# Hybrid pool and mLSTM decode layer on one core: products reordered between units, input copied for the combinations, more row tiles in the heads

## Chip, cores and metric

The kernel runs on one core of a Trainium2 chip. The metric is the device time of one execution in microseconds (us). TensorE is PE in the rows, VectorE DVE, ScalarE ACT, GpSimd POOL, SyncE SP.

## What is computed

One layer on 560 rows of 1024 values: 16 meta tokens and 512 prompt tokens, and 8 sequences of 4 sample tokens. All is fp32. Shortened from the reference:

```python
hn = rmsnorm(x, norm_g)
a_pool, z_pool, q, k, v, o, z_m, i_pre, f_pre, g_pool, g_mlstm = split(hn @ w_in)
y_pool = multiscale_pool(pool_buf, a_pool, w_pool, pool_scale) * silu(z_pool)
# mLSTM, 4 heads of 512: gates ig, lf = log_sigmoid(f); running maximum m
s   = (q @ k.T) * w_intra
num = s @ v + w_inter * (q @ C)
den = sum(s) + w_inter * (q @ n)
h   = num / max(abs(den), exp(-m_t))
C_new = decay * C + (k * w_state).T @ v
y_mlstm = sigmoid(o) * head_norm(h) * silu(z_m)
u = sigmoid(g_pool) * (y_pool @ w_branch_pool) + sigmoid(g_mlstm) * (y_mlstm @ w_branch_mlstm)
y = rmsnorm(x + u @ w_out, final_g)
```

## The kernel before

Each fp32 operand is split into a high part, rounded to fp32r, and the rest, `lo`; a product is three fp32r matmuls (`mm3`, line 161). The hidden rows stand transposed in `hT_hi` and `hT_lo`, 128 by 8 by 560.

**Front.** `begin` normalises five row tiles, transposes them, copies the high part out of the transposes' PSUM banks on ScalarE, subtracts for the low part on VectorE (`parts`, line 445), and runs the first input projection (`project`, line 464) on tiles 0 and 1, then on the others. `projections_begin` (660) weaves three step lists into the v units of head 0 (`unit_v`, 949): the gate weights' products and the gate chain (`gates`, 560), and `quarter_sums` (531).

**Combinations.** Most column blocks of the input projection are *quad* units (`quad`, 186): a two by two block product with seven products p1, p2, p6, p5, p7, p3, p4 in place of eight. They need four combinations S a to d of quarters of the hidden rows. `quarter_sums` rebuilds the input as `hT_hi + hT_lo` on GpSimd (line 539), eight times in two rounds, adds and subtracts on VectorE (542), and splits into high (ScalarE, 549) and low parts (547, b and d on GpSimd). A unit combines its weights too: `ahead` loads `ra` and `rb`, casts `w1` and `w2`, adds, casts `wa` and `wb`, and subtracts the low parts on VectorE.

**Order.** In `projections` (687) the program writes the order of TensorE by hand: unit after unit, each with the next unit's `ahead` steps, the previous unit's `after` steps and the update of the sample state (C) woven in. p2 and p7 to p4 accumulate in PSUM banks which a unit's own evictions (`keep`, `total`) free: p1 into bank A, kept by ScalarE (238), then p6 into A; VectorE forms q, zx and so on from the banks (251, 253, 255), and p4 is the last product in A.

**Heads.** `attention` (1201) runs four heads: scores of query and key, weights P, `key_sums` (D, then its split dh and dl, 1411 to 1416), `numerator` (sqn and og, 1449 to 1456), `variances`, a square root and a reciprocal, and `scaled` (1470), which multiplies og by D and stores it. D, four og and four sqn of a head come from the tag `row` with 9 tiles (1255). `rows` are the products for C_prompt (1358, 1359), called prompt_C below. Then come the pool branch (`yp`, loaded by `y_in`, 1497), the mLSTM branch and the output product.

Of the kernel before, what the change touches and what calls it, by code (L numbers as in the profile page):

```python
# [8 lines left out]
F32 = mybir.dt.float32  # L9
F32R = mybir.dt.float32r  # L10
AF = mybir.ActivationFunctionType
ALU = mybir.AluOpType
# [4 lines left out]
P = 128  # L17
# [66 lines left out]
class Unit:  # L84
# [3 lines left out]
    def __init__(self, load=(), ahead=(), products=(), after=(), then=()):  # L88
        self.load, self.ahead, self.products = list(load), list(ahead), list(products)
        self.after, self.then = list(after), list(then)  # L90


# [7 lines left out]
class Trunk:  # L100
# [85 lines left out]
    def quad(self, src, lo, dst, scale=None, f21=None, after=(), then=()):  # L186
# [94 lines left out]
        def p4():  # L281
            product("A", cols("wb", 0), quarter(1, 1), False)
            for out, c0, c1, how in w["dst"]["21"]:
                A.activation(out, view(w["A"], c0, c1, how), f21 or AF.Copy, scale=1.0 if scale is None else scale)
        return Unit([load], ahead, [p1, p2, p6, p5, p7, p3, p4], after, then)

# [76 lines left out]
    def begin(self):  # L363
# [28 lines left out]
        V.tensor_copy(self.ones, self.ones32)  # L392
        self.hT = [ip.tile([P, NK, NT], F32R, name=n) for n in ("hT_hi", "hT_lo")]
        self.hS = ip.tile([P, NK, 112], F32R, name="hS")
        self.acol = mp.tile([P, 5, H], F32, name="acol")
# [49 lines left out]
        def parts(*js):  # L445
            pieces = []
            for j in js:
                for q in range(2):
                    pv = pss[j, q].rearrange("p (k t) -> p k t", k=4)
                    for s, n, c0 in COLS[j]:  # L450
                        pieces.append((pv[:, :, s:s + n], *(t[:, 4 * q:4 * q + 4, c0:c0 + n] for t in self.hT)))
            for src, hi, lo in pieces:
                pA.copy(hi, src)
            for src, hi, lo in pieces:
                pV.tensor_tensor(lo, src, hi.bitcast(F32), ALU.subtract)

        def first(j):
# [73 lines left out]
    def quarter_sums(self):  # L531
        nc = self.nc
        V, A, G = nc.vector, nc.scalar, nc.gpsimd
        steps, x = [], {}

        def load(k0, half, kh):
            t = x[half, kh] = self.gp.tile([P, 2, HN], F32, tag=f"x{half}{kh}", name=self.name("x"), bufs=1)
            hi, lo = (t[:, 4 * kh + k0:4 * kh + k0 + 2, HN * half:HN * half + HN].bitcast(F32) for t in self.hT)
            G.tensor_tensor(t, hi, lo, ALU.add)  # L539

        def sums(op, out, p, q):
            V.tensor_tensor(x[out], x[p], x[q], op)

        def part(k0, s, t, low):
            hi, lo = (u[:, k0:k0 + 2] for u in self.S[s])
            if low:
                (G if s in "bd" else V).tensor_tensor(lo, x[t], hi.bitcast(F32), ALU.subtract)
            else:
                A.copy(hi, x[t])
        a, b, c, d = (1, 1), (0, 0), (1, 0), (0, 1)  # L550
        for k0 in (0, 2):
            steps += [lambda k0=k0, t=t: load(k0, *t) for t in (a, c, b, d)]
            steps += [lambda: sums(ALU.subtract, a, c, a), lambda: sums(ALU.subtract, c, b, c),
                      lambda: sums(ALU.subtract, b, a, b), lambda: sums(ALU.add, d, d, b)]
            for s, t in ("a", a), ("b", b), ("c", c), ("d", d):
                steps += [lambda k0=k0, s=s, t=t, l=l: part(k0, s, t, l) for l in (False, True)]
        return steps


    def gates(self):  # L560
# [21 lines left out]

        V.scalar_tensor_tensor(az, z, -1.0, z, ALU.mult, ALU.max)
        e, u = row("ge"), row("gu")
# [38 lines left out]
        for i in (3, 2, 1, 0):  # L623
            own = TILE0[i] + P - TSTART[i]
            V.tensor_copy(sv[i][:, :own], nQ[:, TSTART[i]:TSTART[i] + own])

            V.tensor_scalar(sv[i][:, own:], sv[i + 1][:, :SEGW[i] - own],
                            b[:, TILE0[i] + P - 1:TILE0[i] + P], None, ALU.add)
            yield
        for i in range(5):  # L630
            c0 = TILE0[i]
            c1 = c0 + (P if i < 4 else 16)
            last = (SEGW[i] if i < 4 else 16) - 1
            V.tensor_scalar(wsr[:, c0:c1], a[:, c0:c1], sv[i][:, last:last + 1], None, ALU.add)
            yield
# [24 lines left out]
    def projections_begin(self):  # L660
# [6 lines left out]
        sums = self.quarter_sums()  # L667
        for f in v[0].ahead + a.products:
            f()
        for n, u in enumerate(v):  # L670
            now = [sums[:len(sums) // (4 - n)], other[:len(other) // (6 - n)]]
            sums, other = sums[len(now[0]):], other[len(now[1]):]
            if n == 2:
                z = self.unit_z(0)
                for f in z.load:
                    f()
            weave(u.products, (v[n + 1] if n < 3 else z).ahead, *now)
# [9 lines left out]
    def projections(self, rest):  # L687
# [45 lines left out]
        self.early = self.head(0)  # L733
        loaded, C, outs = 0, {}, []
        before = Unit(after=rest[0].after + rest[1].after)
# [4 lines left out]
        for t, u in enumerate(units):  # L740
# [20 lines left out]
        for f in before.after + old.then + before.then + outs:  # L761
            f()
# [186 lines left out]
    def unit_v(self, h):  # L949
# [251 lines left out]
    def attention(self):  # L1201
# [15 lines left out]
        for h, u in enumerate(heads):  # L1217
# [21 lines left out]
    def head(self, h):  # L1239
# [256 lines left out]

    def y_in(self, yy, k, src):
        nc = self.nc
        t = self.r("y32")[:, :NO]
        nc.sync.dma_start(t, src)  # L1500
        self.split(yy[0][:, k], yy[1][:, k], t, nc.scalar, nc.gpsimd if k % 2 else nc.vector)
# [11 lines left out]
    def pool_branch(self):  # L1513
# [12 lines left out]
        for k in range(8):  # L1526
            self.y_in(self.yp2, k, self.yp_d[:, k])
        for g in range(4):
# [7 lines left out]
    def final(self, up):  # L1536
# [4 lines left out]
        for m in range(16):  # L1541
            y_in(ym[m // 8], m % 8, self.y_d[:, m])
        fg = fp.tile([P, D], F32, name="fg")
# [95 lines left out]
```

## Time and profile before

| | us |
|---|---|
| three runs | 1145.27, 1148.51, 1151.25 |
| median | 1148.51 |
| profiled execution | 1146.45 |
| its span | 1144.6 |
| TensorE, VectorE, ScalarE, GpSimd busy | 1066.5, 843.0, 533.5, 195.2 |
| granted TensorE clock, mean | 0.97 |

The busy times lie in the span; what the profiled execution takes beyond its span lies around it. An idle time in brackets in a row is that of the engine just before the instruction, with what ended it; idle time counts only where the engine is the one that sets the end. The granted clock is 1.00 at 2.4 GHz and 0.50 at 1.2 GHz.

### The profile page before, as it was taken

What the parts mean: (1) busy time and instruction counts of PE and PEld (TensorE: products, weight loads), DVE (VectorE), ACT (ScalarE), POOL (GpSimd) and SP (SyncE); (2) the same over time, 40 slices, a digit from 0 to 9 for tenths busy, and PEclk for the clock granted to TensorE, in tenths of its full rate; (3) what the DMA queues carried; (4) which work ended last, traced back from release to release, by engine and by line L of the source; (5) the groups of instructions that cost most, each with busy time, mean ns of one, the idle gap of its engine ahead of it and who ended that gap; (6) DMA issues with size and microseconds to landing.
All of it is one profiled execution on the core that took longest, in us unless ns stands there. A gap on an engine that the chain in (4) does not pass through costs nothing.

```text
span 1144.6 us, 19677 instructions
## 1 busy us (share of the span) xinstructions
PE 1066.5 (93%) x7390; PEld 961.5 (84%) x7390; DVE 843.0 (74%) x1346; ACT 533.5 (47%) x1003; POOL 195.2 (17%) x323
## 2 busy tenths in 40 slices
PE   7948999998999999999998999986999789999997
PEld 5848999967999968999868989975978679999976
DVE  5696888796789697889696888863699888534353
ACT  4455555333554435554444554455677555222232
POOL 3720120001210000400001300022454534100000
PEclk9978999998999999999999999997999899999999
DMA  8424456779656778657588567887677699522232
GB/s 214 149 51 122 136 166 203 256 235 275 214 182 219 238 257 236 212 178 249 186 266 262 167 223 268 282 280 259 205 264 248 203 310 353 174 74 75 66 116 83
DMA packets 159663, 233.33 MB, mean 204 GB/s; under 512 B 17369, under 2 KB 82133, under 8 KB 159561
## 3 DMA queue, kind: packets, MB, share of 16 engines
q1 hardware_dynamic: 159569, 232.09, 63.2%
q8 instruction: 58, 0.95, 0.3%
q14 instruction: 36, 0.29, 0.1%
HBM read 160.65 MB, written 70.93 MB: 202 GB/s over the span
## 4 chain that ended last, share of the span: by engine, by line
PE 68%; DMA 11%; DVE 9%; issue 4%; ACT 3%; POOL 3%; SPq 1%; DVEq 0%; POOLq 0%; ACTq 0%
PE ps L166 55%; PE ps L974 4%; DMA v_d<-v 3%; PE ps L1121 2%; DMA wraw<-in_w_in_dram 2%; PE ps L1358 2%; PE ps L1130 1%; DMA kw<-k_d 1%; DMA out_dram<-C 1%; POOL x L539 1%; ACT qc L1156 1%; DMA k<-k_d 1%; PE ps L1401 1%; PE ps L977 1%; DMA ra<-in_w_in_dram 1%
## 5 line engine op out<-in xcount | busy, mean ns | idle before, releaser
L166 PE MATMUL ps<-hT_hi,w 128*128 128x272 f32 (+1 forms) x752 | 159.0, 297 | 0.0
L166 PEld LDWEIGHTS ps<-hT_hi,w 128*128 128x128 f32 x752 | 125.3, 193 | 4.2 <-issue 2.4
L166 PE MATMUL ps<-hT_lo,w 128*128 128x272 f32 (+1 forms) x376 | 110.2, 293 | 0.0
L1135 DVE SCALAR_TENSOR_TENSOR C<-C,sw,ps 128x512 f32<-128x512 f32 x128 | 89.4, 741 | 12.1 <-PE ps L1130 11.8
L166 PE MATMUL ps<-Sb_hi,wb 128*128 128x272 f32 (+1 forms) x376 | 80.9, 295 | 17.5 <-DVE wb L205 15.6
L166 PE MATMUL ps<-hT_hi,wb 128*128 128x272 f32 (+1 forms) x376 | 82.7, 299 | 11.4 <-DVE q L253 7.7
L1044 POOL COPY qm<-qw 128x16 f32<-128x16 f32 x32 | 7.1, 254 | 430.4 <-DVE qw L1041 430.4
L166 PE MATMUL ps<-Sa_hi,wa 128*128 128x272 f32 (+1 forms) x376 | 79.9, 292 | 0.0
L166 PE MATMUL ps<-Sc_hi,wa 128*128 128x272 f32 (+1 forms) x376 | 78.9, 290 | 0.0
L166 PEld LDWEIGHTS ps<-Sb_hi,wb 128*128 128x128 f32 x376 | 63.2, 192 | 18.7 <-issue 16.0
L166 PE MATMUL ps<-Sd_hi,w 128*128 128x272 f32 (+1 forms) x376 | 78.7, 289 | 0.0
L202 ACT CAST wa<-ra 128x1024 fp32r<-128x1024 f32 x47 | 49.4, 1050 | 62.0 <-DVE ra L215 55.4
L205 DVE TENSOR_TENSOR wb<-rb,wb 128x1024 fp32r<-128x1024 f32 x47 | 57.7, 1227 | 24.6 <-ACT wb L202 24.3
L166 PEld LDWEIGHTS ps<-hT_hi,wb 128*128 128x128 f32 x376 | 64.5, 195 | 13.1 <-DVE q L253 8.4
L166 PEld LDWEIGHTS ps<-hT_lo,w 128*128 128x128 f32 x376 | 72.6, 193 | 0.0
L202 ACT CAST w<-rb 128x1024 fp32r<-128x1024 f32 x47 | 49.3, 1050 | 29.3 <-PE ps L166 16.2
L166 PEld LDWEIGHTS ps<-Sa_hi,wa 128*128 128x128 f32 x376 | 63.0, 191 | 0.0
L166 PEld LDWEIGHTS ps<-Sc_hi,wa 128*128 128x128 f32 x376 | 62.2, 189 | 0.0
L166 PEld LDWEIGHTS ps<-Sd_hi,w 128*128 128x128 f32 x376 | 61.9, 188 | 0.0
L205 DVE TENSOR_TENSOR w<-rb,w 128x1024 fp32r<-128x1024 f32 x47 | 57.3, 1220 | 4.3 <-ACT w L202 4.3
L205 DVE TENSOR_TENSOR wa<-ra,wa 128x1024 fp32r<-128x1024 f32 x47 | 57.5, 1224 | 0.0
L166 PE MATMUL ps<-hT_lo,wb 128*128 128x272 f32 (+1 forms) x188 | 55.8, 297 | 0.0
(372 smaller groups left out, 3115.6 us busy)
## 6 DMA issues: line engine op xcount, KB each, us to landing
C<-in_state_C_dram SPq DMA_DIRECT2D x64, 512.0 KB
out_dram<-C SPq DMA_DIRECT2D x64, 512.0 KB
ra<-in_w_in_dram SPq DMA_DIRECT2D x47, 512.0 KB
rb<-in_w_in_dram SPq DMA_DIRECT2D x47, 512.0 KB
wraw<-in_w_in_dram SPq DMA_DIRECT2D x18, 512.0 KB
v<-v_d SPq DMA_DIRECT2D x32, 256.5 KB
wraw<-in_w_branch_mlstm_dram SPq DMA_DIRECT2D x16, 512.0 KB
k_d<-k SPq DMA_DIRECT2D x16, 280.0 KB
```

Source lines behind the costliest of these rows:

```text
L166: self.nc.tensor.matmul(out, s, m, start=(first and j == 0), stop=(j == len(seq) - 1), skip_group_check=not check)
L202: A.copy(w[name][0], w[s])
L205: V.tensor_tensor(w[name][1], w[s], w[name][0].bitcast(F32), ALU.subtract)
L539: G.tensor_tensor(t, hi, lo, ALU.add)
L974: nc.tensor.matmul(pv[i], s, m[:, k2], start=(k == 0 and j == 0), stop=(k == 7 and j == 2))
L977: nc.tensor.matmul(pv[4][:112], self.hS[:, k], m[:, k2], start=(k == 0 and j == 0), stop=(k == 7 and j == 1))
L1121: nc.tensor.matmul(self.pqc[h][r:r + 8], self.qm[h % 2][:, d, b], Cs[bb // 2][:, bb % 2], start=(d == 0 and g == 0), stop=(d == 3 and g == 1),
L1130: nc.tensor.matmul(pu, self.kwst[h, d][r:r + 12, g], self.vst[h][r:r + 12, g], start=True, stop=True, tile_position=(r, 0))
L1135: V.scalar_tensor_tensor(C, C, self.bview(self.sw[h][:, 0])[:, 4 * g + bb, 3:4], pu, ALU.mult, ALU.add)
L1156: A.activation(t[r, :HD], pqc[r], AF.Copy, accum_out=t[r, HD:])
L1358: nc.tensor.matmul(pc, w[:, s, i], vr[i][:, m], start=(i == 0 and j == 0), stop=False)
L1401: nc.tensor.matmul(pb[:, o:o + mv.shape[-1] - m], s, mv[:, m:], start=(j == 0), stop=(j == last[True]))
```

## The change

1. **Tails.** A quad unit's last product, p4, is issued behind the first product of the unit after it, where that unit's first product is an ordinary one.
2. **Input X.** The transposes' banks are copied whole by ScalarE into a tile X, after the high and low parts; `quarter_sums` takes quarters of X, in place. All low parts of S, and those of the first v unit's weights, are VectorE's. Around the gates, the absolute value, four copies and five adds of the gate rows are ScalarE's, and the first four gate steps stand ahead of the v units.
3. **Heads.** 13 row tiles; the last prompt_C behind the last head's numerators; the first two loads of the pool branch's input ahead of them.

```diff
-        return Unit([load], ahead, [p1, p2, p6, p5, p7, p3, p4], after, then)
+        u = Unit([load], ahead, [p1, p2, p6, p5, p7, p3, p4], after, then)
+        u.tail = True
+        return u
...
-            for src, hi, lo in pieces:
+            for src, hi, lo, x in pieces:
                 pA.copy(hi, src)
-            for src, hi, lo in pieces:
+            for src, hi, lo, x in pieces:
                 pV.tensor_tensor(lo, src, hi.bitcast(F32), ALU.subtract)
+            for src, hi, lo, x in pieces:
+                pA.copy(x, src)
...
-        def load(k0, half, kh):
-            t = x[half, kh] = self.gp.tile([P, 2, HN], F32, tag=f"x{half}{kh}", name=self.name("x"), bufs=1)
-            hi, lo = (t[:, 4 * kh + k0:4 * kh + k0 + 2, HN * half:HN * half + HN].bitcast(F32) for t in self.hT)
-            G.tensor_tensor(t, hi, lo, ALU.add)
+        def quarter(k0, half, kh):
+            x[half, kh] = self.X[:, 4 * kh + k0:4 * kh + k0 + 2, HN * half:HN * half + HN]
...
-                (G if s in "bd" else V).tensor_tensor(lo, x[t], hi.bitcast(F32), ALU.subtract)
+                V.tensor_tensor(lo, x[t], hi.bitcast(F32), ALU.subtract)
...
-        V.scalar_tensor_tensor(az, z, -1.0, z, ALU.mult, ALU.max)
+        nc.scalar.activation(az, z, AF.Abs)
...
-            V.tensor_copy(sv[i][:, :own], nQ[:, TSTART[i]:TSTART[i] + own])
+            nc.scalar.copy(sv[i][:, :own], nQ[:, TSTART[i]:TSTART[i] + own])
...
-            V.tensor_scalar(wsr[:, c0:c1], a[:, c0:c1], sv[i][:, last:last + 1], None, ALU.add)
+            nc.scalar.activation(wsr[:, c0:c1], a[:, c0:c1], AF.Identity, bias=sv[i][:, last:last + 1])
...
-        for f in v[0].ahead + a.products:
+        for f in v[0].ahead + a.products + other[:4]:
             f()
+        other = other[4:]
...
             products = u.products
+            for f in products[:1] + tail:
+                f()
+            products, tail = products[1:], []
+            if u.tail:
+                products, tail = products[:-1], products[-1:]
             if t not in values:
-
-                products, extra = products[:1] + extra + products[1:], []
+                products, extra = extra + products, []
...
-                (G if h == 0 and kk % 2 else V).tensor_tensor(w[kk][2], w[kk][0], w[kk][1].bitcast(F32), ALU.subtract)
+                V.tensor_tensor(w[kk][2], w[kk][0], w[kk][1].bitcast(F32), ALU.subtract)
...
-                weave(u.rows[-2:], u.sums, last)
-            weave(u.numerators[:-1] if h == H - 1 else u.numerators, m.keys + m.values)
+                weave(u.rows[-2:-1], u.sums, last)
+            if h == H - 1:
+                self.yraw = [self.y_load(self.yp_d[:, k]) for k in range(2)]
+                weave(u.numerators[:-1] + u.rows[-1:])
+            else:
+                weave(u.numerators, m.keys + m.values)
...
-            return self.hp.tile([P, NO], F32, tag="row", name=self.name(name), bufs=9)
+            return self.hp.tile([P, NO], F32, tag="row", name=self.name(name), bufs=13)
```

ScalarE in the front, before, from the first cast of row tile 2 (hT_hi, from the transposes' banks `ps`) to the first weights of the v unit (`whi`):

```order
L80 CAST hT_hi<-ps_244 128x4x128
L80 CAST hT_hi<-ps_249 128x4x128
L80 CAST hT_hi<-ps_262 128x4x128
L80 CAST hT_hi<-ps_267 128x4x128
L80 CAST hT_hi<-ps_297 128x4x24 x2
L80 CAST hT_hi<-ps_302 128x4x24 x2
L137 CAST wg<-wg_raw 128x8x64
L961 CAST whi_408<-wraw_120 128x1024
```

The same place in the change:

```order
L80 CAST hT_hi<-ps_267 128x4x128
L80 CAST hT_hi<-ps_272 128x4x128
L80 COPY X<-ps_249 128x4x128
L138 CAST wg<-wg_raw 128x8x64
L80 COPY X<-ps_254 128x4x128
L80 COPY X<-ps_267 128x4x128
L80 COPY X<-ps_272 128x4x128
L80 CAST hT_hi<-ps_302 128x4x24 x2
L80 CAST hT_hi<-ps_307 128x4x24 x2
```

The cast of the gate weights moved from behind the last row tile's casts to a place ahead of them, with three copies between.

TensorE at the end of the first q unit of head 1, before: the last two matmuls of p3 (`Sd`), then p4 (`hT`, `wb`), whose bank is `ps_2892`:

```order
L166 MATMUL ps_2952<-Sd_lo,w_424_2777 128x272
L166 MATMUL ps_2952<-Sd_hi,w_424_2777 128x272
L166 MATMUL ps_2892<-hT_hi,wb_2838 128x272
L166 MATMUL ps_2892<-hT_lo,wb_2837 128x272
L166 MATMUL ps_2892<-hT_hi,wb_2837 128x272
```

And in the change, where `w_435` is w1 of the next q unit:

```order
L167 MATMUL ps_2952<-Sd_hi,w_417_2780 128x272
L167 MATMUL ps_3017<-hT_hi,w_435_2858 128x272
L167 MATMUL ps_3017<-hT_lo,w_435_2858 128x272
L167 MATMUL ps_3017<-hT_hi,w_435_2858 128x272 x2
L167 MATMUL ps_3017<-hT_lo,w_435_2858 128x272
L167 MATMUL ps_3017<-hT_hi,w_435_2858 128x272 x2
L167 MATMUL ps_3017<-hT_lo,w_435_2858 128x272
L167 MATMUL ps_3017<-hT_hi,w_435_2858 128x272 x2
L167 MATMUL ps_3017<-hT_lo,w_435_2858 128x272
L167 MATMUL ps_3017<-hT_hi,w_435_2858 128x272
L167 MATMUL ps_2888<-hT_hi,wb_2835 128x272
L167 MATMUL ps_2888<-hT_lo,wb_2834 128x272
```

The twelve matmuls of the next unit's p1 stand between p3 and p4; this is so in 35 of the 47 quad units.

TensorE at the end of the heads in the change: the last two numerator rows, prompt_C (line 1372 here, 1358 before), a transpose and the pool branch:

```order
L1415 MATMUL ps_10786<-Ph_10653,vc_10606 128x144
L1415 MATMUL ps_10786<-Ph_10653,vc_10627 128x48 x2
L1372 MATMUL ps_10817<-vr_10027,kwr_10237 128x512 x3
L1372 MATMUL ps_10817<-vr_10032,kwr_10237 128x512 x3
L1372 MATMUL ps_10817<-vr_10069,kwr_10237 128x512 x3
L1372 MATMUL ps_10817<-vr_10074,kwr_10237 128x512 x3
L1373 MATMUL ps_10817<-vpt_8828,kwst_10240 128x512
L1242 MATMUL ps_10834<-ident,npr 16x128
L167 MATMUL ps_10909<-yp_10853,wlo_10858 128x272
```

Before, these thirteen matmuls stood ahead of the last head's first numerator.

## Rows read from the trace of the kernel before

**Rows 1.** The page, busy time by engine: us, share of the span, instructions.
```profile
PE 1066.5 (93%) x7390; PEld 961.5 (84%) x7390; DVE 843.0 (74%) x1346; ACT 533.5 (47%) x1003; POOL 195.2 (17%) x323
```

**Rows 2.** Busy time by stretch: start:end, length, engines, granted clock, DMA share, GB/s.
```profile
20.00:95.00 75.00, 55.01 (x308) 48.38 (x309) 56.55 (x90) 33.93 (x73) 31.36 (x25) 0.89 0.44 117
277.14:283.20 6.06, 6.06 (x27) 6.06 (x27) 4.54 (x8) 2.28 (x4) 2.12 (x7) 0.50 1.00 317
885.00:940.00 55.00, 41.80 (x282) 39.48 (x281) 43.85 (x61) 28.43 (x59) 21.24 (x29) 0.88 0.72 242
```

**Rows 3.** TensorE's waits: for what, us in total, times, longest us.
```profile
PE ps L166 <- DVE wb L205: 15.6, 1, 15.6
PE ps L1399 <- DVE dl L140: 8.5, 1, 8.5
PE ps L166 <- DVE q L253: 7.7, 3, 3.5
...
PE ps L166 <- ACT yp L137: 4.7, 1, 4.7
...
PE ps L166 <- DVE zx L253: 3.0, 1, 3.0
...
PE ps L166 <- ACT p L238: 1.8, 3, 0.6
```

**Rows 4.** Chain that ended last, 20 to 96 us: start us, us, what.
```profile
32.63 3.69 POOL x L539 x2
...
81.60 5.63 DMA v_d<-v
87.24 6.51 DMA v_d<-v
```

**Rows 5.** Timeline of VectorE: start us, us, instruction, [idle before <- releaser].
```profile
39.63 5.25 DVE L542 TENSOR_TENSOR x<-x,x 128x560 f32<-128x560 f32 x4 [5.92 <-POOL x L539]
...
61.35 0.72 DVE L542 TENSOR_TENSOR x<-x,x 128x560 f32<-128x560 f32 x1
...
273.65 0.69 DVE L140 TENSOR_TENSOR vsp<-v,vsp 32x512 fp32r<-32x512 f32 x1 [5.01 <-DMA v_d<-v]
274.37 0.69 DVE L212 TENSOR_TENSOR w<-ra,w 128x512 fp32r<-128x512 f32 x1
```

**Rows 6.** Timeline of TensorE, the same columns.
```profile
26.53 0.41 PE L80 MATMUL ps<-hT_lo,whi 128*128 128x304 f32 x1 [0.92 <-DVE hT_lo L80]
...
33.30 0.47 PE L974 MATMUL ps<-whi,hT_lo 128*128 128x512 f32 x1
...
82.70 0.57 PE L166 MATMUL ps<-Sb_hi,wb 128*128 128x272 f32 x1 [15.61 <-DVE wb L205]
...
94.67 0.39 PE L166 MATMUL ps<-hT_hi,wb 128*128 128x272 f32 x1 [3.00 <-DVE zx L253]
...
277.14 0.60 PE L166 MATMUL ps<-hT_hi,wb 128*128 128x272 f32 x1 [2.65 <-DVE q L253]
...
444.48 0.39 PE L166 MATMUL ps<-hT_hi,wb 128*128 128x272 f32 x1 [1.60 <-DVE q L253]
...
446.09 0.29 PE L166 MATMUL ps<-hT_hi,w 128*128 128x272 f32 x1
```

**Rows 7.** Timeline of ScalarE, the same columns.
```profile
30.63 0.62 ACT L137 CAST wg<-wg_raw 128x512 fp32r<-128x512 f32 x1 [5.90 <-DMA wg_raw<-in_w_in_dram]
...
62.79 1.28 ACT L588 ACT_TABLE_LOAD   x1
64.08 0.67 ACT L588 ACTIVATE lf<-gu 4x560 f32<-4x560 f32 x1
```

**Rows 8.** Timeline of GpSimd in the heads, the same columns.
```profile
893.68 1.45 POOL L1411 TENSOR_TENSOR D<-bc 128x400 f32<-128x400 f32 x1 [3.17 <-DVE og L1470]
```

**Rows 9.** Timeline of TensorE in the heads, the same columns.
```profile
917.88 2.88 PE L1358 MATMUL ps<-vr,kwr 128*128 128x512 f32 x12
920.60 0.39 PE L1359 MATMUL ps<-vpt,kwst 96*128 96x512 f32 x1
```

**Rows 10.** The page, costliest groups: busy, mean ns, idle before, releaser.
```profile
L202 ACT CAST w<-rb 128x1024 fp32r<-128x1024 f32 x47 | 49.3, 1050 | 29.3 <-PE ps L166 16.2
```

More of the change, by code (lines that the diff above doesn't have):

```diff
@@ L90, in __init__ @@
         self.after, self.then = list(after), list(then)
+        self.tail = False
 def weave(*lists):
@@ L393, in begin @@
         self.hT = [ip.tile([P, NK, NT], F32R, name=n) for n in ("hT_hi", "hT_lo")]
+        self.X = gp.tile([P, NK, NT], F32, name="X")
         self.hS = ip.tile([P, NK, 112], F32R, name="hS")
@@ L450, in parts @@
                     for s, n, c0 in COLS[j]:
-                        pieces.append((pv[:, :, s:s + n], *(t[:, 4 * q:4 * q + 4, c0:c0 + n] for t in self.hT)))
-            for src, hi, lo in pieces:
+                        pieces.append((pv[:, :, s:s + n], *(t[:, 4 * q:4 * q + 4, c0:c0 + n] for t in (*self.hT, self.X))))
+            for src, hi, lo, x in pieces:
                 pA.copy(hi, src)
-            for src, hi, lo in pieces:
+            for src, hi, lo, x in pieces:
                 pV.tensor_tensor(lo, src, hi.bitcast(F32), ALU.subtract)
+            for src, hi, lo, x in pieces:
+                pA.copy(x, src)
         def first(j):
@@ L551, in quarter_sums @@
         for k0 in (0, 2):
-            steps += [lambda k0=k0, t=t: load(k0, *t) for t in (a, c, b, d)]
-            steps += [lambda: sums(ALU.subtract, a, c, a), lambda: sums(ALU.subtract, c, b, c),
+            steps += [lambda k0=k0: [quarter(k0, *t) for t in (a, c, b, d)], lambda: sums(ALU.subtract, a, c, a), lambda: sums(ALU.subtract, c, b, c),
                       lambda: sums(ALU.subtract, b, a, b), lambda: sums(ALU.add, d, d, b)]
@@ L733, in projections @@
         self.early = self.head(0)
-        loaded, C, outs = 0, {}, []
+        loaded, C, outs, tail = 0, {}, [], []
         before = Unit(after=rest[0].after + rest[1].after)
@@ L755, in projections @@
             products = u.products
+            for f in products[:1] + tail:
[3 more added lines that the diff above has]
+                products, tail = products[:-1], products[-1:]
             if t not in values:
-                products, extra = products[:1] + extra + products[1:], []
+                products, extra = extra + products, []
             weave(products, ahead, old.then + before.after, extra, done, self.gate_steps[t] if t < 2 else [])
             old, before = before, u
-        for f in before.after + old.then + before.then + outs:
+        for f in tail + before.after + old.then + before.then + outs:
             f()
@@ L1495, in both, with y_load, y_in @@
         return [pool.tile([P, 8, NO], F32R, tag="yy", name=f"{name}{j}", bufs=bufs) for j in range(2)]
-    def y_in(self, yy, k, src):
+    def y_load(self, src):
+        t = self.r("y32")[:, :NO]
+        self.nc.sync.dma_start(t, src)
+        return t
+    def y_in(self, yy, k, t):
         nc = self.nc
-        t = self.r("y32")[:, :NO]
-        nc.sync.dma_start(t, src)
         self.split(yy[0][:, k], yy[1][:, k], t, nc.scalar, nc.gpsimd if k % 2 else nc.vector)
@@ L1526, in pool_branch @@
         for k in range(8):
-            self.y_in(self.yp2, k, self.yp_d[:, k])
+            self.y_in(self.yp2, k, self.yraw[k] if k < 2 else self.y_load(self.yp_d[:, k]))
         for g in range(4):
@@ L1541, in final @@
         for m in range(16):
-            y_in(ym[m // 8], m % 8, self.y_d[:, m])
+            y_in(ym[m // 8], m % 8, self.y_load(self.y_d[:, m]))
         fg = fp.tile([P, D], F32, name="fg")
```

## The prediction

> **What bounds the kernel now.** I read the busy shares first, then the busy time by stretch, then the list of what TensorE waits for, and only then the engines behind each wait. TensorE works 1066.5 us of the 1144.6 us span [rows 1], so what can be won without removing matmuls is some 78 us of idle time and what the clock loses after it. The stretches say where much of that lies: from 20 to 95 us TensorE is idle for 20.0 us, with a mean granted clock of 0.89; from 885 to 940 us for 13.2 us, at 0.88 [rows 2]. The list of waits names the ends: 15.6 us for wb, 8.5 for dl, three times q with 7.7 in all, 4.7 for yp, 3.0 for zx, three times p with 1.8 in all [rows 3]. These sum to 41.3 us, and the change touches the place of every one of them.
>
> The profiled execution took 1146.45 us: 1.85 us more than its span, 2.06 us less than the median of the three runs, 1148.51. My sum is made against 1146.45. A measurement of this kernel can tell a difference of about 0.5%, 5.7 us, from none.
>
> **Front, 20 to 95 us.** In the chain that sets this stretch POOL, once it has split the gate weights, spends 3.69 us on its first two input sums x [rows 4], and DVE can add only at 39.63. Its four adds take 5.25 us there, while POOL works too, against 0.72 us for one such add at 61.35 [rows 5]. The gate chain, and wb_lo behind it, end so late that p6 of the first z unit starts at 82.70, after 15.61 us of idle time: p1 and p2 had ended at 67.09 [rows 6].
>
> *Removed:* eight sums on POOL and its low parts. *Added:* twelve copies X on ScalarE (the larger ones the size of the 0.62 us cast of wg [rows 7], so 7 us at most, in time that was idle), and on DVE four S_lo of some 0.72 us, like the adds, and two wlo. DVE has the room: it now waits for POOL until 39.63 [rows 5].
>
> *Moved, and it costs:* ScalarE takes its work in order, and the cast of wg, which starts only at 30.63, when its DMA has landed [rows 7], now stands ahead of three copies X and of hT_hi of the last row tile. With 0.62 us for it, three copies of 0.5 and the small casts, and hT_lo on DVE behind them, I put the last tile's projection at 33.9 instead of 26.53 [rows 6]. That is an idle stretch of some 6.5 us which before did not have, and 2.5 us for the clock after it (the size it had after a shorter wait, below). The work from there to the v units is 6.8 us (26.53 to 33.30 [rows 6]): it ends at 43.2 instead of 33.3. Gates and v units took from 33.30 to 63.9 (67.09 less two products of 1.61 us each, 444.48 to 446.09 [rows 6]), 30.6 us; the gates' first four steps now come in one run, with nothing removed, so v ends at 73.8, and p1 and p2 at 77.0. This is 9.9 us *later* than before, and falls into the 15.6 us that were idle.
>
> *What ends the wait then:* the gate chain on DVE runs without POOL beside it and is over well before; wb's cast on ScalarE stands behind the copies of v, some 3 us, and ends near 76.9, DVE's low part takes 1.2. So p6 starts at 78.1 instead of 82.70. From 82.70 to the next wait TensorE took 8.97 us (94.67 less 3.00 [rows 6]) for four products, which at full clock are 6.4 us: p3 ends at 84.5. *Late next:* the first zx on DVE, which frees p4's bank and now stands behind landings of v_d and vs_d stores. Two store landings, 5.63 and 6.51 us one behind the other, lead to zx in the chain of before [rows 4]; from about 76 on, when v is copied, that gives 88, though the stores meet less other traffic. I put p4 at 87.5. Against 94.67 the front gains **7.2 us**; bounds 0 (the stores land as late as now) and 11 (p4 follows p3, and the 0.85 us lost to the clock behind 94.67 go too).
>
> **Tails, 95 to 753 us.** In the order 35 of the 47 quad units have p4 behind the next unit's p1. Three times p4 waits for q on DVE, 2.65 us at 277 and 1.60 us at 444 [rows 6], 3.5 us the longest [rows 3]. DVE itself is held there by landings of v_d, 5.01 us at 273.65, and the next unit's w1_lo stands right behind that wait, at 274.37 [rows 5]. So at 277 the next p1 could start near 275.1, 0.6 us after p3's end, and with its 1.6 us end before q is there: it covers 1.6 us of each wait, 4.8 us in all, and two pieces under 1 us each are left of the one at 277. Behind the 2.65 us wait the granted clock is 0.50, 1.2 GHz, from 277.14 to 283.20 [rows 2]: 26 matmuls (a 27th starts as the stretch ends) take 6.06 us where at 1.61 us for twelve they would take 3.5, so 2.6 us are lost. Behind the 1.60 us wait they keep to 1.61 us, the pace of 2.4 GHz [rows 6]. So I count the 2.6 us as won, and nothing for the clock behind the third wait, of which 1.9 us remain. The three waits for p, 0.6 us each [rows 3], go as well, since p4 now stands between p1 and p6: 1.8 us. Sum **9.2 us**; bounds 1.8 (the store holds p1 as long as p4) and 11.
>
> **Heads, 753 to 940 us.** POOL's D waits 3.17 us at 893.68 for DVE's og of the head before [rows 8], because it takes the row tile of that head's D, which these products read. With 13 tiles it has another; the wait goes and dl follows earlier. The 8.5 us for dl shrink, but not to nothing: DVE is busy 43.85 of 55 us in this stretch [rows 2]. I take 4.5 us, D's 3.2 and some of what DVE does out of turn now. The last prompt_C, 2.88 us and one matmul more [rows 9], leaves its place at 917.88 and goes behind the last numerators, into the 4.7 us for yp [rows 3]; the first two y loads are issued before it, so that yp comes no later: 2.7 us. *Added:* two table loads on ScalarE for the heads. One takes 1.28 us at 62.79 and the next ACTIVATE starts at 64.08 [rows 7]: 2.6 us in all, of which I take 1.2 as exposed. Sum **6.0 us**; bounds 0 (DVE sets the end either way) and 13.2 (both waits go).
>
> For a table switch the Trainium skill, "ScalarE: Activation LUTs", section "What ACT_TABLE_LOAD costs", counts 2.66 us, a load of 1.28 and a drain of 1.38. By it the two would cost 5.3 us, and the heads would give up to 2.7 us less; the trace agrees on the load and shows no drain beside it, and the measurement decides. Section "Rules for kernel authors" of the same page speaks against one part of the change: an add belongs on VectorE, not on ScalarE. Nine short copies and adds of gate rows go the other way here; no row of before shows them on ScalarE.
>
> Those nine I cost at nothing: ScalarE waits for other engines in the front, and DVE's chain gets shorter by them; uncovered they would be some 3 us. From 940 us on nothing changes. **Sum:** 7.2 + 9.2 + 6.0 = 22.4 us, so 1146.45 - 22.4 = 1124.05, **1124 us**.
>
> **Rivals.**
> 1. *The stores take the front's place.* If v_d and vs_d land as late as now, zx holds p4 to 93 and the front gives 1 or 2 us: 1130. For it: zx waits 3.0 us today [rows 3], and more landings stand ahead of it in DVE's order. Against: v's copies no longer wait behind the gate chain. Chance 0.17.
> 2. *The heads are DVE's.* If D comes earlier but dl doesn't, the heads give 0: 1130. For it DVE's 43.85 us [rows 2], against it that the chain to dl runs over D. Chance 0.13.
> 3. *The tails move the wait.* If w1_lo is held as long as q, p1 waits in p4's place, the clock falls as before and tails give 1.8: 1131. For it: 274.37 lies behind 273.65 [rows 5]; against: only by 0.7 us. Chance 0.08.
> 4. *Two of these together:* 1136 to 1146, half of it within 0.5% of before. Chance 0.08.
> 5. *Slower: the weight tiles run short.* p4 is wb's last reader and now frees it 1.6 us later. ScalarE's casts of w already wait 16.2 us for TensorE over 47 units [rows 10]. If each of 35 tails makes a next cast, and with it p6, late by 0.9 us, 31.5 us are lost against 22.4 won: 1155. Below 0.8 us per unit it is not slower by 5.7. Against: in the order the casts wait for p7 and p3 of older units, none for a moved p4. Chance 0.06.
>
> **Numbers.** The forecast has the rest, 0.48. All upper bounds together give 1111 (11 + 11 + 13.2); the range begins there, takes in rivals 1 to 3 and half of 4, and ends at 1140. Faster by over 0.5%, below 1140.7: 0.48 + 0.17 + 0.13 + 0.08, less 0.02 for their tails, 0.84. Within: 0.10. Slower: 0.06.
>
> **What would show it.** p6 of the first z unit near 78 with under 2 us idle before it; a new idle stretch of some 6 us between 26 and 34 us; no wait for q over 2 us, and no slow stretch behind the first; no D of POOL waiting for og; under 2 us for yp. Wrong would be: v ending after 76, zx held over 4 us, a p6 that waits in every unit, dl still 8 us late.

## The result and the profile after

The changed kernel took 1130.3 us in the median (four runs, 1128.91 to 1132.77), the kernel before beside it 1149.8: a ratio of 0.984, 95% interval 0.980 to 0.988. Run again later, with five runs, it took 1134.1, ratio 0.988 (0.986 to 0.990). So it is faster by 1.2 to 1.6%, 14 to 19 us, inside the range, where 22.4 us were forecast. The two profiled executions have spans of 1127.2 and 1128.7 us, against 1144.6.

The busy shares of the changed kernel, on its page:

```profile
PE 1062.4 (94%) x7390; PEld 957.6 (85%) x7390; DVE 826.4 (73%) x1342; ACT 542.7 (48%) x1027; POOL 155.1 (14%) x309
```

Against [rows 1] GpSimd lost 40.1 us and VectorE 16.6, ScalarE got 9.2 more. TensorE's 7390 matmuls are the same and take 4.1 us less. The other 13.3 us of the span's 17.4 are idle time of TensorE, so its list of waits is read next (what it waits for, us in total, times, longest):

```profile
PE ps L80 <- ACT hT_hi L80: 8.9, 2, 6.6
PE ps L167 <- ACT u L239: 7.9, 2, 4.1
...
PE ps L1359 <- DVE kw L1341: 4.3, 2, 2.3
...
PE ps L167 <- DVE q L254: 3.5, 3, 1.7
...
PE ps L167 <- DVE wlo L141: 3.1, 1, 3.1
PE ps L1413 <- DVE sl L141: 2.7, 1, 2.7
...
PE ps L167 <- ACT p L239: 1.9, 2, 1.4
```

Beside [rows 3]: wb's 15.6 us, zx's 3.0, dl's 8.5 and yp's 4.7 are gone as such, q's 7.7 are 3.5. In their places stand hT_hi, which was forecast, and **u**, 7.9 us, kw and sl in the heads, and wlo, 3.1 us, at the product that waited for yp, which were not.

Where the gain lies along the program is seen by taking the start of the same product in both traces and subtracting. The first product on S_a of a unit serves as a mark; a mark's time in the kernel before stands at the left, and the lead of each kernel over it in us. Each column is one execution. The two of the changed kernel differ by 1.3 to 3.9 us in the same row, so a difference of that size between two columns says little.

| mark in before | changed | again | w1 late | wg late | both late | no tails | w1 late, no tails | old front | low parts on GpSimd | 9 tiles | prompt_C back | old heads | late, old heads |
|---|---|---|---|---|---|---|---|---|---|---|---|---|---|
| 104.6 (front over) | 11.9 | 13.3 | 11.5 | 16.0 | 16.4 | 10.4 | 10.5 | 0.4 | 6.8 | 13.2 | 11.5 | 11.7 | 16.0 |
| 286.0 | 17.5 | 21.1 | 18.6 | 19.0 | 20.9 | 14.4 | 13.4 | 7.0 | 13.6 | 21.0 | 19.9 | 16.3 | 21.9 |
| 308.4 | 12.5 | 14.6 | 19.5 | 12.7 | 21.8 | 10.6 | 13.4 | 0.1 | 9.1 | 15.2 | 15.3 | 10.1 | 22.9 |
| 473.2 | 9.0 | 12.9 | 21.6 | 10.3 | 24.3 | 9.8 | 13.3 | -2.3 | 7.3 | 12.9 | 12.7 | 9.8 | 24.9 |
| 754.4 (projections over) | 10.8 | 12.8 | 21.2 | 11.5 | 25.1 | 8.5 | 10.9 | -1.7 | 7.7 | 13.3 | 14.0 | 10.4 | 24.4 |
| from there to TensorE's last instruction (before: 383.9) | 377.3 | 380.8 | 382.3 | 381.3 | 383.2 | 384.1 | 383.1 | 384.0 | 386.6 | 386.6 | 383.5 | 381.7 | 385.6 |

The first column of numbers tells the story: 11.9 us are won in the front, 5.6 more by the second q unit of head 1 (17.5 at the mark 286.0), and then 5.0 go at one place and 5.3 at a like place in the next head (14.3 at the mark 462.4, 9.0 at 473.2). The other 6.6 us of the profile lie behind the projections; the column of the same kernel run again has 3.1 there.

*The front.* TensorE's timeline after (start, length, instruction, idle before), with the zx that frees p4's bank, on VectorE:

```profile
33.91 0.62 PE L80 MATMUL ps<-hT_hi,whi 128*128 128x304 f32 x1 [6.55 <-ACT hT_hi L80]
...
78.47 0.39 PE L167 MATMUL ps<-Sb_hi,wb 128*128 128x272 f32 x1 [1.42 <-ACT p L239]
...
85.17 0.29 PE L167 MATMUL ps<-hT_hi,wb 128*128 128x272 f32 x1
```
```profile
84.30 0.42 DVE L254 TENSOR_TENSOR zx<-e,ps 128x272 f32<-128x272 f32 x1
```

The new idle time of 6.55 us and p6 at 78.47 behind 1.42 us are what was forecast. But zx has no bracket: nothing held it. p4, the row at 85.17, follows p3 at once, and no wait for zx is left in the list.

*The lost stretch.* Head 1's first key unit, on TensorE, and by stretch (start:end, length, busy time of PE, PEld, DVE, ACT, POOL, granted clock, DMA share, GB/s), then ScalarE in front of it:

```profile
284.98 0.40 PE L167 MATMUL ps<-Sc_hi,wa 128*128 128x280 f32 x1 [4.14 <-ACT u L239]
```
```profile
284.98:289.00 4.02, 4.02 (x20) 4.02 (x21) 3.13 (x6) 1.29 (x2) 0.00 (x0) 0.61 0.87 271
277.00:290.00 13.00, 8.86 (x57) 8.64 (x57) 6.82 (x12) 3.92 (x8) 1.48 (x8) 0.87 0.89 285
```
```profile
284.00 0.62 ACT L210 CAST w<-ra 128x512 fp32r<-128x512 f32 x1 [5.70 <-DMA ra<-in_w_in_dram]
284.53 0.40 ACT L239 ACTIVATE u<-ps 128x280 f32<-128x280 f32 x1
```

u is p6's result in bank A, kept by ScalarE so that p7 may write there. p6 ended at 279.30 (its last matmul began at 279.00 and took 0.30); u stands behind the cast of w1 for the unit two further on, and that cast waits 5.70 us for its load. The same pair of rows stands at 452.53 (5.32 us) and 453.05. In the kernel before the cast waited too, but TensorE was not there yet:

```profile
296.71 0.62 ACT L209 CAST w<-ra 128x512 fp32r<-128x512 f32 x1 [0.89 <-DMA ra<-in_w_in_dram]
297.80 0.40 ACT L238 ACTIVATE u<-ps 128x280 f32<-128x280 f32 x1 [0.47 <-PE ps L166]
```

There u waited for TensorE; now TensorE waits for u. The cast moved 12.71 us to the front, about as far as the front's gain (11.9 at the first mark); TensorE moved by 17.5.

*The heads.* TensorE in the fourth head of the changed kernel, and what VectorE did ahead of sl:

```profile
898.54 0.35 PE L1413 MATMUL ps<-sl,ones 128*128 128x240 f32 x1 [2.65 <-DVE sl L141]
...
918.99 0.39 PE L167 MATMUL ps<-yp,wlo 128*128 128x272 f32 x1 [3.15 <-DVE wlo L141]
```
```profile
870.00:898.00 28.00, 24.39 (x162) 22.46 (x160) 24.92 (x38) 20.17 (x41) 10.85 (x21) 0.94 0.69 222
```

VectorE is busy for 24.92 of the 28 us up to just before TensorE gets sl.

### The profile page after: what moved, and what is told of

Read it like the earlier page. It is cut to its first block, busy times and chain, and to the rows that moved or that the text cites. A ratio compares the mean times of both kernels' runs of the same rounds, so it can differ in the third digit from the quotient of the medians.

```text
span 1127.2 us, 19656 instructions
## 1 busy us (share of the span) xinstructions
PE 1062.4 (94%) x7390; PEld 957.6 (85%) x7390; DVE 826.4 (73%) x1342; ACT 542.7 (48%) x1027; POOL 155.1 (14%) x309
## 4 chain that ended last, share of the span: by engine, by line
PE 76%; DMA 12%; DVE 4%; ACT 3%; issue 2%; SPq 1%; POOL 1%; POOLq 0%; DVEq 0%; ACTq 0%
PE ps L167 57%; PE ps L984 7%; PE ps L1131 3%; PE ps L1372 2%; DMA wraw<-in_w_in_dram 2%; PE ps L1140 2%; DMA v_d<-v 1%; DMA rb<-in_w_in_dram 1%; DMA ra<-in_w_in_dram 1%; PE ps L987 1%; DMA v<-v_d 1%; DMA k<-k_d 1%; PE ps L1415 1%; PE ps L80 1%; ACT qc L1166 1%
## 5 line engine op out<-in xcount | busy, mean ns | idle before, releaser
L1145 DVE SCALAR_TENSOR_TENSOR C<-C,sw,ps 128x512 f32<-128x512 f32 x128 | 89.5, 742 | 10.6 <-PE ps L1140 10.2
L167 PE MATMUL ps<-hT_hi,wb 128*128 128x272 f32 (+1 forms) x376 | 79.7, 291 | 3.5 <-DVE q L254 3.5
L203 ACT CAST wb<-rb 128x1024 fp32r<-128x1024 f32 x47 | 49.1, 1046 | 15.6 <-DVE rb L216 15.4
```

Of the source, the lines that this page charges most:

```text
L167: self.nc.tensor.matmul(out, s, m, start=(first and j == 0), stop=(j == len(seq) - 1), skip_group_check=not check)
L203: A.copy(w[name][0], w[s])
L1145: V.scalar_tensor_tensor(C, C, self.bview(self.sw[h][:, 0])[:, 4 * g + bb, 3:4], pu, ALU.mult, ALU.add)
```

## The experiments

All are measured against the kernel before on the same chip; the table above has their leads.

**1. The late cast.** ScalarE's w1 cast of the unit two further on is pinned (kept in the order in which the program writes it) behind the keep of p1 of the unit ahead of it, at the two places where a wait for u came.

```diff
-            A.copy(w["1"][:, 0], block("a", 0))
+            (Pinned(self.tc, A) if pin.get("cast") else A).copy(w["1"][:, 0], block("a", 0))
...
+            if t in (room[1] - 1, room[2] - 1):
+                u.pin["keep"] = units[t + 1].pin["cast"] = True
```

> One edit on the changed kernel: in two places (heads 1 and 2) ScalarE's cast of the weights w1 for the unit two ahead stands behind the kept p1 of the unit in between, no longer ahead of the kept u of the unit that runs. Theory A (the new waits of 4.14 and 3.77 us of TensorE for u are ScalarE's order: a cast that waits 5.7 and 5.3 us for its weights' DMA, two units early, holds a copy that is due): both waits and the slow clock behind them go, some 5.9 and 5.4 us, span near 1116 to 1118. Theory B (this stretch is bound by the weights' and states' DMA, and the order only shows where): the wait reappears within the next two or three units as a wait of p1 or p6 for weights, span within 3 us of 1127.

1125.4 us, ratio 0.981 (0.978 to 0.984), span 1121.8. Both waits for u are gone; ScalarE now takes u first (its timeline, then the stretch as above):

```profile
278.32 0.41 ACT L239 ACTIVATE u<-ps 128x280 f32<-128x280 f32 x1 [1.09 <-PE ps L167]
```
```profile
277.00:290.00 13.00, 13.00 (x103) 13.00 (x102) 7.42 (x20) 3.79 (x9) 4.52 (x16) 1.00 0.95 288
```

TensorE, idle or slow in this stretch in the changed kernel (8.86 us busy, clock 0.87), works through it at full clock. The lead when the projections end is 21.2 us in place of 10.8 and 12.8: by the traces the two waits, 4.14 and 3.77 us in the first profile, cost 8.4 to 10.4 us with the clock behind them. That is theory A in mechanism, and no wait of theory B appears. The span, 1116 to 1118 in theory A, was missed by some 4 us, since the stretch behind the projections is 382.3 us here. In the time the gain is smaller and less sure: the interval lies below that of the changed kernel's second measurement (0.986 to 0.990) and overlaps that of the first (0.980 to 0.988).

**2. No tails, without and with the late cast.** p4 goes back into its own unit.

```diff
-        u.tail = True
+        u.tail = False
```

> One edit on the changed kernel: the last product of a unit is issued inside its own unit again. Theory A (tails win 4.3 us at the first q unit of heads 1 and 2 and 1.6 at head 3, and the cast that waits for its DMA gives the first two back because the landing does not move): the start of the unit behind k0 stays within 1.5 us of the changed kernel's at 308 and 473 us of before, and the span is only 1 to 3 us longer, 1128 to 1130. Rival (the tails are worth what they remove, and the u waits come from the tails' order itself): without tails the u waits go too, and the span is 1 to 4 us shorter; or, if the u waits stay at 4 us, the span is 7 to 10 us longer.

1138.1 us, 0.992 (0.989 to 0.994). In the projections only 2.3 us go (8.5 against 10.8; 4.3 against the second profile's 12.8), as the theory had it, though the whole lost more, as the rival had it; the rest lies behind the projections (384.1 us against 377.3 and 380.8). Without tails TensorE waits for u over 0.6 us at one place only (its timeline):

```profile
286.88 0.60 PE L167 MATMUL ps<-Sc_hi,wa 128*128 128x280 f32 x1 [2.02 <-ACT u L239]
```

This left open whether the tails are worth little or are eaten by the wait for u, so the last run took them out beside the late cast:

> The kernel with the late w1 cast and without the tails: each pair's last product back in its place, front and heads as changed. The lead over the kernel before at the projections' last product was 21.2 us with both and 8.5 with neither. Theory (the tails are worth the 9 to 10 us that their waits held, once u no longer waits for the cast): the lead there is 11 to 12.5 us and the span near 1132. Rival (the late cast alone brings the gain, the tails little): the lead stays at 18 to 21 us and the span near 1123.

1136.9 us, 0.991 (0.988 to 0.993), span 1132.9; the lead at the end of the projections is 10.9. So with the cast out of the way the tails are worth 21.2 - 10.9 = 10.3 us there, and the late cast without them 10.9 - 8.5 = 2.4, which is within what two executions of one kernel differ by. The theory holds, within what single traces can tell. The times agree: with the late cast the ratio is 0.981 (0.978 to 0.984) with tails and 0.991 (0.988 to 0.993) without, and without tails the late cast changes nothing (0.992 against 0.991). The tails bring TensorE early to u, and most of their gain in the projections is then spent waiting for it. In the time of the whole the changed kernel keeps more of it, 4 to 9 us (0.988 and 0.984 against 0.992); what exceeds the leads lies behind the projections and is not explained.

**3. The cast of wg late, and both.** The cast which holds hT_hi of the last row tile is pinned behind it.

```diff
-        self.split(wg[:, :, 0:64], wg[:, :, 64:128], raw, A, G)
+        pA.copy(wg[:, :, 0:64], raw)
+        G.tensor_tensor(wg[:, :, 64:128], raw, wg[:, :, 0:64].bitcast(F32), ALU.subtract)
```

> One edit on the changed kernel: ScalarE's cast of the gate weights is held in program order behind the casts and copies of the last row tile. Theory A (the 6.55 us idle of TensorE at 33.9 is that cast's wait for its DMA, and the front is now bound by TensorE up to the first z unit): the idle goes, p6 of the first z unit starts 5 to 9 us earlier, span 1118 to 1122. Rival (VectorE's sums, low parts and gate chain set the first z unit, so that the idle only moves in front of p6): p6 moves by under 2 us and a wait for wb of 5 us or more returns, span 1126 to 1128.

The new idle time shrinks from 6.55 to 1.63 us, p6 of the first z unit starts at 74.06, 4.4 us earlier (theory A had 5 to 9), and the lead at 104.6 is 16.0. But the time is 1129.8, 0.985 (0.981 to 0.989), no better than the changed kernel, and the span of the profile, 1130.5, misses theory A's 1118 to 1122: p6 of the unit behind the mark 104.6 waits, by the pattern of the lost stretch, for a kept p that stands behind a cast which waits for a load (TensorE, then ScalarE, timelines).

```profile
99.78 0.39 PE L167 MATMUL ps<-Sb_hi,wb 128*128 128x272 f32 x1 [1.98 <-ACT p L239]
```
```profile
98.39 1.04 ACT L203 CAST w<-rb 128x1024 fp32r<-128x1024 f32 x1 [2.59 <-DMA rb<-in_w_in_dram]
99.34 0.39 ACT L239 ACTIVATE p<-ps 128x272 f32<-128x272 f32 x1
```

> Both edits together, on the changed kernel. If both theories A hold and the gains add, 1107 to 1112 span; if a front that comes earlier only runs sooner into the DMA of heads 1 and 2, no more than the better of the two alone, 1116 to 1120.

1122.7 us, 0.980 (0.976 to 0.985), span 1118.8, with a lead of 25.1 when the projections end, 3.9 more than the late w1 alone. Its interval overlaps that of the late w1 alone (0.978 to 0.984).

**4. The front as before.** Order of the sums, gates, start of the projections and first v unit undone; tails and heads as changed.

```diff
-        for f in v[0].ahead + a.products + other[:4]:
+        for f in v[0].ahead + a.products:
...
+            G.tensor_tensor(t, hi, lo, ALU.add)
```

> The changed kernel with the front as it was before (order of the quarter's sums, their gates, the start of the first projection and the first v unit), the tails and heads as changed. Theory (the front's 12 us pass unshortened to the end): span about 12 us longer, near 1139, and the waits for u in the second and third projection head stay near 4 us, as their loads shift with TensorE. Rival (a part of the front's gain is given back at the waits for u): those waits shrink below 1 us and the span is only 6 to 8 us longer, near 1134.

1148.3 us, 0.999 (0.997 to 1.000), span 1146.5: tails and heads alone are worth nothing that can be measured. Against the first profile the front is worth 11.5 us at 104.6 and 12.5 at the end of the projections. The theory's second half holds as well, the waits for u do not shrink. TensorE's timeline in head 1:

```profile
296.80 0.60 PE L167 MATMUL ps<-Sc_hi,wa 128*128 128x280 f32 x1 [5.47 <-ACT u L239]
```

That the span lost 19.3 us (17.8 against the second profile) and not 12 lies for the greater part behind the projections, again (384.0 us).

**5. Low parts back on GpSimd.** S_b and S_d, and the odd weights of the first v unit.

```diff
-                V.tensor_tensor(lo, x[t], hi.bitcast(F32), ALU.subtract)
+                (G if s in "bd" else V).tensor_tensor(lo, x[t], hi.bitcast(F32), ALU.subtract)
```

> The changed kernel with the low parts of the sums S_b and S_d and the odd low parts of the first v unit's weights back on GpSimd. Theory A (GpSimd's and VectorE's work side by side slow one another, and p6 of the first z unit came late for that): p6 comes 3 to 6 us later than 78.5 us and the span grows by as much, to 1130 to 1133. Rival (the front's gain comes from the order of the work, and p6 waits for ScalarE's p alone): p6 stays within 1 us of 78.5 and the span within 1 us of 1127.

1139.9 us, 0.991 (0.988 to 0.994). The lead at 104.6 falls from 11.9 to 6.8 and p6 comes 2.8 us later, near theory A in size, but by another way; the span, 1139.6, is 6.6 us above its range. VectorE's two adds beside GpSimd's S_b_lo are not slowed (41.92, 0.69 us apiece): there it is GpSimd's subtraction that takes 5.52 us, and 1.39 right after, with VectorE idle for most of it. wb_lo, at 75.85, is even 0.34 us earlier than in the changed kernel. VectorE, GpSimd and ScalarE of this kernel:

```profile
41.92 1.38 DVE L546 TENSOR_TENSOR X<-X 128x560 f32<-128x560 f32 x2
...
50.38 2.04 DVE L973 TENSOR_TENSOR wlo<-wraw,whi 128x1024 fp32r<-128x1024 f32 x1 [0.50 <-ACT whi L971]
...
54.25 2.78 DVE L216 TENSOR_TENSOR ra<-ra 128x512 f32<-128x512 f32 x1
```
```profile
40.16 5.52 POOL L551 TENSOR_TENSOR Sb_lo<-X,Sb_hi 128x560 fp32r<-128x560 f32 x1 [4.63 <-ACT Sb_hi L553]
45.64 1.39 POOL L551 TENSOR_TENSOR Sb_lo<-X,Sb_hi 128x560 fp32r<-128x560 f32 x1
...
53.63 2.85 POOL L973 TENSOR_TENSOR wlo<-wraw,whi 128x1024 fp32r<-128x1024 f32 x1
```
```profile
79.88 1.04 ACT L203 CAST w<-rb 128x1024 fp32r<-128x1024 f32 x1
80.83 0.38 ACT L239 ACTIVATE p<-ps 128x272 f32<-128x272 f32 x1
```

p6 comes at 81.26, behind 4.49 us for p, which ScalarE here takes behind a split of v and two casts of the next unit's weights, where the changed kernel took it at 78.05 ahead of them. Behind that wait the granted clock is 0.54 from 81.26 to 87.30, where the changed kernel has 1.00 behind its 1.42 us; with it the 2.8 us become the 5.1 of the lead. So some 5 us of the front's gain hang on where p stands in ScalarE's order. VectorE beside GpSimd is slowed most at two places: 2.78 us for an add of weights that takes 0.69 in the changed kernel, and 2.04 for a subtraction of wlo that takes 1.22.

**6. The heads part by part.** Nine row tiles; then the last prompt_C back; then the whole part undone.

```diff
-            return self.hp.tile([P, NO], F32, tag="row", name=self.name(name), bufs=13)
+            return self.hp.tile([P, NO], F32, tag="row", name=self.name(name), bufs=9)
```

> The changed kernel with 9 instead of 13 row tiles in the heads, nothing else. Theory (the 13 tiles are what took TensorE's wait for the combinations' tiles away): the wait for a row tile before the third head's transposes comes back at 3 to 8 us, the gain over the kernel before at the third head's combinations falls from 21 us to about 13, and the span is 3 to 5 us longer than the changed kernel's 1127.2, near 1131. Rival (VectorE sets the end of the heads, the tiles only move where TensorE waits): the wait comes back but the span is within 1 us of 1127.

1135.4 us, 0.987 (0.983 to 0.991), span 6.8 us longer than that of the changed kernel's first profile and 5.3 longer than that of its second. The wait for dl is back with 7.06 us, and the one for wlo is 5.95 us. By the spans that is the theory's direction and more than its 3 to 5 us, but the intervals of the ratios overlap.

```diff
-                weave(u.rows[-2:-1], u.sums, last)
+                weave(u.rows[-2:], u.sums, last)
...
-                weave(u.numerators[:-1] + u.rows[-1:])
+                weave(u.numerators[:-1])
```

> The changed kernel with the last prompt combination's products back in their former place among the sums, the loads of y left where the change put them. Theory (they fill TensorE's wait ahead of the last head's products): the wait there grows from 3.15 us to about 6, and 2 to 3 us of the gain go: span near 1130. Rival (the wait is for a VectorE operation that itself waits for TensorE's numerators, and so comes earlier when they do): the wait stays near 3 us and the span within 1 us of 1127.

1132.0 us, 0.985 (0.981 to 0.988). The wait is 5.18 us in place of 3.15, so the product covers 2.0 us of it, as forecast in kind; in the time nothing of that can be measured.

> The changed kernel with the heads as they were before (9 row tiles, both last prompt combinations among the sums, the loads of y late); front and tails as changed. Theory (the heads' part is worth its 8 us on the path): span 7 to 9 us longer, near 1135, with the waits for dl of 7 to 8 us back. Rival 1 (the other kernels show the heads worth 0 to 3 us): span 1128 to 1131, dl's wait back but the waits for sl and kw gone. In both, the projections' gain at their last product stays near 10.8 us.

1133.8 us, 0.987 (0.984 to 0.989), against 0.988 (0.986 to 0.990) for the changed kernel in the same runs: **the heads' part is worth nothing that can be measured**, though its waits come back as they were (timelines of TensorE and GpSimd, then the stretch ahead of dl with the columns as above):

```profile
890.97 0.54 PE L1409 MATMUL ps<-dl,ones 128*128 128x240 f32 x1 [8.22 <-DVE dl L141]
922.84 0.82 PE L167 MATMUL ps<-yp,wlo 128*128 128x272 f32 x2 [4.71 <-ACT yp L138]
```
```profile
881.30 1.46 POOL L1421 TENSOR_TENSOR D<-bc 128x400 f32<-128x400 f32 x1 [2.56 <-DVE og L1480]
```
```profile
863.00:890.50 27.50, 18.62 (x123) 17.05 (x123) 25.85 (x38) 20.15 (x41) 16.90 (x26) 0.84 0.71 227
```

VectorE is busy for 25.85 of the 27.5 us ahead of dl, and for 24.92 of the 28 ahead of sl in the changed kernel. By these shares it is the bound of this stretch either way; no run gave VectorE less work there, so that is read and not tested. In one kernel TensorE meets it mainly once, for 8.22 us; in the other at kw (2.33), st (1.04) and sl (2.65 us), with smaller waits between. From the projections' last product on S_a to the pool branch's first product it is 175.5 and 176.9 us in the two profiles of the changed kernel, 178.9 here and 181.0 in the kernel before. Other kernels with the changed heads take up to 182.8 (low parts on GpSimd), so these 2 to 3 us cannot be told from chance either.

**7. Late casts with the heads as before.**

> The kernel with both casts late, the fastest so far, with the heads as before. Theory: the heads are worth 8 us, so the span is near 1127 against 1118.8. Rival: they are worth 0 to 3 us, span 1119 to 1122. If the time is lower than 1122 us, this is the best kernel and the heads' part is worth nothing.

1122.9 us, 0.979 (0.976 to 0.982): its ratio is the lowest of all, with an interval that overlaps nearly the whole of that of both casts late (1122.7, 0.976 to 0.985), and it does without the heads' part. By the span of its profile, 1122.3, the rival holds but for 0.3 us.

**8. The changed kernel once more.**

> The changed kernel once more, unaltered. In its profile the stretch from the last product of the projections to the end was 6 to 9 us shorter than in the kernel before and in every kernel of the experiments, and the granted clock stayed at 1.00 after a wait of 3.15 us for wlo, after which it fell in the others. Theory (chance of one execution): the clock falls this time, and that stretch is 2 to 4 us longer; median near 1131. Rival (belongs to the program): the stretch is within 1 us of 377 us again and the clock stays at 1.00 there.

1134.1 us, and the stretch behind the projections 380.8 us, 3.5 longer than in the first profile. The 6 us right behind the wait for wlo show a part of why, first in the first profile, then in the second:

```profile
918.99:924.99 6.00, 6.00 (x48) 6.00 (x48) 5.25 (x5) 3.92 (x8) 3.54 (x3) 1.00 0.96 312
```
```profile
918.40:924.40 6.00, 6.00 (x35) 6.00 (x36) 4.87 (x5) 3.79 (x8) 3.71 (x3) 0.72 1.01 344
```

After nearly the same wait (3.15 and 3.14 us) TensorE did 48 matmuls at full clock in the one and 35 in the other. So part of the 6.6 us that the first profile shows behind the projections is one execution's chance; the other kernels stand at 381 to 387 us there, and what orders them was not settled.

## Why the forecast was right in sign and too high in size

*Front: right in mechanism, too small.* 7.2 us were forecast, 11.9 and 13.3 came by the mark 104.6 (10.4 without tails). p1 and p2 end at 77.05 (forecast 77.0), p6 starts at 78.47 (78.1), the last tile's projection at 33.91 (33.9). The step that failed is the zx that was to stand "behind landings of v_d and vs_d stores": VectorE took zx at 84.30 without idle time, and p4 came at 85.17, 9.5 us earlier than before, and not at 87.5. The case of the upper bound, p4 following p3 and the clock won too, is what happened, and its clock term was too small as well: 0.85 us were put on it, and from p4 to the mark TensorE took 9.90 us before and 7.45 after (stretches before, then after):

```profile
94.67:104.57 9.90, 9.90 (x57) 9.59 (x58) 8.69 (x17) 5.26 (x9) 0.00 (x0) 0.66 0.17 42
```
```profile
85.17:92.62 7.45, 6.83 (x55) 6.42 (x53) 7.09 (x15) 5.58 (x8) 0.00 (x0) 1.00 0.10 27
```

I had carried the two landings of the old chain [rows 4] over. In the changed kernel the last v_d store is issued at 75.81 and not at 87.24, and the zx that waited stands ahead of the second split of v in VectorE's order; which of the two took the wait away was not tried. Rival 1 is refuted by the missing wait.

*Tails: right in kind, near in size, and taken back elsewhere.* 9.2 us were forecast from covered waits and the clock; with the w1 cast out of the way they are 10.3. That it comes so near is in part luck: 2.6 of the 10.3 are there by the mark 269.8, ahead of the three waits for q, where the forecast counted nothing. The wait for q that was 2.65 us [rows 6] is 1.09, all three are 3.5 in place of 7.7 (forecast 2.9), and the clock behind the first is 1.00 where it was 0.50 [rows 2] (stretch behind p4 at 263.86):

```profile
263.86:269.92 6.06, 6.06 (x48) 6.06 (x49) 4.91 (x6) 3.29 (x6) 0.00 (x0) 1.00 0.98 288
```

That clock is no sure work of the tails: without them it was 1.00 behind a wait of 1.56 us at the same place, and 0.72 behind 1.93 us without them and with the late cast. In the changed kernel only 2.3 us arrive (4.3 by its second profile). The step that failed is one that is missing: the sum asked what each tail covers, and not what is late next once TensorE is 17.5 us early. It was ScalarE's cast of w1, which waits for its own load, and u behind it. Rival 3 had a wait take the tails' gain, though at p1 and for w1_lo; rival 5 feared casts, though for their tiles, and neither was this one.

*Heads: wrong.* 6.0 us were forecast, none can be measured. The step that failed is the 4.5 us for dl: D comes earlier, no D waits for og any more and the wait for dl is gone, but VectorE, busy for most of the stretch, holds TensorE at kw, st and sl instead. That was rival 2, with a chance of 0.13. Of the 2.7 us for prompt_C, 2.0 show at the wait itself, which is 3.15 us and so not under the 2 that were to show it. The two added table loads are there, six in the heads in place of four, 1.28 us each (ScalarE's groups by line: busy, mean ns, idle before):

```profile
L1325 ACT ACT_TABLE_LOAD x3 | 3.8, 1283 | 0.4 <-DMA bc<-rows_d 0.4
L1481 ACT ACT_TABLE_LOAD x3 | 3.8, 1283 | 0.1
```

The Trainium skill, "ScalarE: Activation LUTs", section "What ACT_TABLE_LOAD costs", counts a drain beside the load; no row here shows one: the load at 76.18 ends at 77.46 and the next ACTIVATE starts at 77.47, and so it is, 0.01 us behind the load, at nine of the kernel's ten loads.

*The sum.* +4.7 in the front, -6.9 to the tails and -6.0 for the heads would leave 14.2 us won; measured were 14 to 19. The parts do not add up so well along the program: the lead when the projections end is 10.8 and 12.8 us, and 6.6 and 3.1 us come behind them, where the heads' part brings nothing that can be measured and the cause stays open. That 22.4 came as near as it did is luck to that extent: the front gave more than forecast where tails and heads gave less.

## What to carry to other kernels

Pulling an engine ahead pulls it towards every wait that its helpers spent unseen. Before counting a covered wait as won, look in the helper's in-order queue for an instruction that waits for a load (here a cast two units ahead of its need) and ask what stands behind it; by the leads, pinning that one cast behind the urgent copy was worth more (8.4 to 10.4 us) than the tails brought without it (2.3 to 4.3). Where one engine is busy for about 90% of a whole stretch (here 89 and 94%), taking a wait for it away in one place can bring it back in another.

## What the runs showed of the hardware that was not expected

The granted clock behind a wait is no function of the wait's length alone. In two executions of the same program a wait of 3.15 us left it at 1.00 and one of 3.14 us was followed by 0.72 over 6 us (above). Near the end, TensorE waits for wolo 1.25 us in the kernel before and 1.27 us, to 1070.27, in the changed one; the clock stays at 1.00 in the 6 us behind the first, with 26 matmuls, and is 0.72 behind the second, with 19 (before, then after):

```profile
1089.32:1095.32 6.00, 6.00 (x26) 4.58 (x27) 3.50 (x4) 3.56 (x4) 0.22 (x2) 1.00 0.71 236
```
```profile
1070.27:1076.27 6.00, 6.00 (x19) 4.58 (x20) 3.74 (x4) 3.14 (x3) 0.22 (x2) 0.72 0.70 222
```

Which of two such cases will come I could not tell from a trace, so a clock loss behind a short wait belongs into the range rather than the sum. And GpSimd's work beside VectorE slows sometimes the one and sometimes the other. Of the four adds in the kernel before [rows 5] only the first is slow, while GpSimd subtracts for wlo (2.40 us from 39.55); the other three take 0.74 us each, with GpSimd idle:

```profile
39.63 2.92 DVE L542 TENSOR_TENSOR x<-x,x 128x560 f32<-128x560 f32 x1 [5.92 <-POOL x L539]
```

So the prediction read four slow adds where there was one. In experiment 5 two adds keep 0.69 us and GpSimd's S_b_lo, which started while VectorE was at work, takes 5.52; 12 us later an add of VectorE, which started while GpSimd was at work, takes 2.78.
